# A macaron block's mixer re-ordered: attention A in pairs of row halves beside B's projections, B's attention beside half of the output projection

## The chip, the cores and the metric

The kernel runs on one core of a Trainium2 chip. A core has TensorE (PE in the profile; PEld is its weight load), VectorE (DVE), ScalarE (ACT), GpSimd (POOL) and SyncE (SP, which issues the DMAs). The metric is the device time of one execution in microseconds (us); the time of a kernel is the median of its runs.

## What is computed

One Conformer block on x of 512 rows and 1024 columns, in float32:

```python
x = x + 0.5 * swiglu(rmsnorm(x, ffn1_norm), ffn1_w_gate, ffn1_w_up, ffn1_w_down)
proj = rmsnorm(x, mix_norm) @ w_in          # qa | ka | va | c_q | c_kv | k_rope
qa, ka = rmsnorm per head of 64 (8 heads);  va as it is
out_a = chunked_relbias_attention(qa, ka, va, a_rel_bias)
# B: q = rmsnorm(c_q) @ w_uq (8 heads of 64 + 32), kv = rmsnorm(c_kv) @ w_ukv (8 heads of 64 + 64);
# each part of q and k normed per head, the 32 columns rotated (rope)
out_b = mla_attention(c_q, c_kv, k_rope, ..., w_uq, ..., w_ukv, ...)
x = x + concatenate([out_a, out_b]) @ w_out
x = x + 0.5 * swiglu(rmsnorm(x, ffn2_norm), ffn2_w_gate, ffn2_w_up, ffn2_w_down)
x = rmsnorm(x, final_norm)
```

Both attentions are causal in chunks of 64 rows. A adds a learned bias to the scores, B only the mask.

## The kernel before

Every float32 operand of a product is split into a high part (rounded to the matmul's own type) and a low part (the rest), and `mm3` (L146) makes a product of three matmuls: high by high, high by low, low by high. A weight comes in by `wunit` (L136): one DMA into a `raw` tile (four of them), a copy on ACT for the high part, a subtraction on POOL, or on DVE where `lo_on` says so, for the low part. `whi` and `wlo` have four buffers each.

The kernel has three stages: FFN1 (L207 to L244), the mixer (L248 to L578) with the output projection (L589 to L599), and FFN2. The change is in the middle stage, which lies between 367.6 us and 622.8 us of the profiled span. Its order before:

- `in_proj` (L314) makes four PSUM banks (one for each 128 rows) of one slice of `w_in`. The slices come in this order: the latents (L334), A's queries (`qk_proj`, L377), A's keys (L433), A's values (`values_proj`, L442). PSUM has 8 banks; `bank` (L309) gives a projection four of the banks that the attention will use, in two groups.
- Between A's queries and A's keys stand B's projections: `latents_T` (L358) transposes the normed latents into `latT`; L384 to L404 make B's queries in 8 steps (six matmuls, a copy on ACT, a square on POOL, L396, two sums on DVE, L397 and L398), then the norms (`factors`, L276) and on POOL the scaling (L403) and `rope` (L291, seven POOL instructions, L294 to L304); L407 to L431 make B's keys and values in 8 steps, with a square (L420) and the scaling of the keys (L431) on POOL. The low parts of these weights are made on DVE.
- `factors` calls `rsqrt` (L112): a Ln and an Exp on ACT, each with a table load, and four small DVE instructions.
- The loop at L569 runs over 16 heads, A's eight and then B's eight. For a head, `front` (L468) transposes queries and keys and splits them (`evac`, L460), and for A loads the bias by a DMA and turns its sign on DVE (L482); `softmax` (L507) makes four blocks of scores and for each the bias and the minimum on DVE (L522), the exponential on ACT (L524), the reciprocal on DVE (L525) and the scaling on POOL (L526); `flip` (L529) transposes the probabilities (L542) and splits them on ACT and DVE (L547, L548); `values` (L552) multiplies with the values. In one turn the loop issues the flip of a head, the softmax of the next, the front of the one after, and the values of the one before.
- A's score matmuls use 64 rows of the array: heads with an even number the lower half of the partitions, heads with an odd number the upper half.
- The output projection (L589) has eight steps of 24 matmuls. After each come the residual sum (L595), the split of the new x for FFN2 (L596, L597) and its square (L599, `add_square`).

The framework orders each engine's instructions when the kernel is built, from a priority by the program's order (`high_priority(offset=150)` puts some ahead) and a model of when operands are there. On the chip each engine runs its own list in that order.

Of the kernel before, what the change touches and what calls it, by code (L numbers as in the profile page):

```python
# [11 lines left out]
F32R = mybir.dt.float32r  # L12
AF = mybir.ActivationFunctionType
# [4 lines left out]
P = 128  # L18
# [12 lines left out]
BIG = 1e30  # L31

# [7 lines left out]
def tile_macaron_block(  # L40
# [206 lines left out]
    AH, AL = XH, XL  # L247
    with tc.tile_pool(name="mix", bufs=1, side="left", reuse_waits="tile") as mp:  # L248
        latT = mp.tile([P, 6, S], F32R, tag="vAh", name="latT")
        VBh = mp.tile([P, NT, 4, 192], F32R, tag="vBh", name="VBh")  # L250
        qA = mp.tile([P, NT, 512], F32, tag="qA", name="qA")
        VBl = mp.tile([P, NT, 4, 192], F32R, tag="vBl", name="VBl")
        kA = mp.tile([P, NT, 512], F32, tag="kA", name="kA")
# [3 lines left out]
        for t in (VBh, VBl):  # L257
            pool.memset(t[:, :, :, HD:2 * HD].bitcast(F32), 0.0)
# [6 lines left out]
        rtmp = mp.tile([P, 2560], F32, tag="vAl", name="rtmp")  # L265
        qt = rtmp[:, 0:2048].rearrange("p (t h w) -> p t h w", t=NT, h=NH)
        rtab = rtmp[:, 2048:2560].rearrange("p (i t n w) -> p i t n w", i=2, t=NT, n=4)
# [5 lines left out]
        dve.tensor_scalar(out=nq[:, 0:1], in0=g(C_AQ), scalar1=-(HD ** -0.5), scalar2=None, op0=ALU.mult)  # L273
        dve.tensor_scalar(out=nq[:, 1:2], in0=g(C_BQ), scalar1=-(QK ** -0.5), scalar2=None, op0=ALU.mult)

        def factors(ss, n, width, scaled, name):  # L276

            f = mp.tile([P, NT, n], F32, tag="f_" + name, name="f_" + name)
            y = mp.tile([P, NT, n], F32, tag="y_" + name, name="y_" + name)
            y2 = mp.tile([P, NT, n], F32, tag="z_" + name, name="z_" + name)  # L280
            if scaled:
                dve.tensor_tensor(out=f, in0=ss, in1=vtok.unsqueeze(2).broadcast_to([P, NT, n]), op=ALU.mult)
                dve.tensor_scalar(out=f, in0=f, scalar1=1.0 / width, scalar2=EPS, op0=ALU.mult, op1=ALU.add)
            else:
                dve.tensor_scalar(out=f, in0=ss, scalar1=1.0 / width, scalar2=EPS, op0=ALU.mult, op1=ALU.add)
            rsqrt(f, f, y, y2)
            if scaled:
                dve.tensor_tensor(out=f, in0=f, in1=rtok.unsqueeze(2).broadcast_to([P, NT, n]), op=ALU.mult)
            return f
# [16 lines left out]
        with tc.tile_pool(name="ps2", bufs=1, space=PSUM, reuse_waits="tile") as ps:  # L306
            NB = {"s": 2, "tr": 2, "t": 3, "pv": 1}

            def bank(group, i, name):  # L309

                tag = (("s",) * NB["s"] + ("tr",) * NB["tr"], ("t",) * NB["t"] + ("pv",) * NB["pv"])[group][i]
                return ps.tile([P, 512], F32, tag=tag, name=name, bufs=NB[tag])

# [20 lines left out]
            pts = in_proj(0, LAT, 1)  # L334
            mt = bank(0, 3, "mt")
# [3 lines left out]
            yt = mp.tile([P, NT], F32, tag="yt", name="yt")  # L339
            zt = mp.tile([P, NT], F32, tag="zt", name="zt")  # L340
            rsqrt(rtok, vtok, yt, zt)
# [5 lines left out]
            fcq = factors(ssl[:, 0], 1, 256, True, "cq")  # L347
            fkv = factors(ssl[:, 1], 1, 128, True, "ckv")
            fkr = factors(ssl[:, 2], 1, 32, True, "kr")
# [5 lines left out]
            kt = mp.tile([P, NT, 1, 64], F32, tag="kt", name="kt")  # L355
            rope(kpe[:, :, HD:QK].unsqueeze(2), lat[:, :, 384:416].unsqueeze(2), fkr, 1, 1, kt)

            def latents_T():  # L358
                for j in range(3):
                    pt = bank(1, j, "lt")  # L360
                    for t in range(NT):
                        pe.transpose(pt[:, t * P:(t + 1) * P], lat[:, t, j * P:(j + 1) * P], ident)
                    act.activation(latT[:, 2 * j, :], pt, AF.Copy, scale=g(C_QLAT + j))
                    dve.scalar_tensor_tensor(out=latT[:, 2 * j + 1, :], in0=pt, scalar=g(C_QLAT + j),
                                             in1=latT[:, 2 * j, :].bitcast(F32), op0=ALU.mult, op1=ALU.subtract)

            def qk_proj(off, dst, name):
                pts = in_proj(off, 512, 0)
# [3 lines left out]
                f = factors(ss, NH, HD, True, name)  # L372
# [3 lines left out]

            qk_proj(416, qA, "qa")  # L377
            latents_T()


            qB = mp.tile([P, NT, NH, QK], F32, tag="qB", name="qB")
            ssn = mp.tile([P, NT, NH], F32, tag="ssn", name="ssn")
            ssp = mp.tile([P, NT, NH], F32, tag="ssp", name="ssp")
            for half in range(2):  # L384
                hi, lo = wunit(w_uq[half], 768, dve)
                for t in range(NT):
                    tt = slice(t * P, (t + 1) * P)
                    pt = bank(1, t, "uq")
                    for k in range(2):
                        c = slice(k * 384, (k + 1) * 384)  # L390
                        mm3(pt[:, :384], latT[:, 2 * k, tt], latT[:, 2 * k + 1, tt], hi[:, c], lo[:, c], k == 0, k == 1)
# [44 lines left out]
            def values_proj():  # L436
# [3 lines left out]
                for t in (VAh, VAl):  # L440
                    pool.memset(t[:, :, :, HD:2 * HD].bitcast(F32), 0.0)
# [299 lines left out]
```

## Time and profile before

| what | us |
|---|---|
| median of 3 runs (995.2 to 997.3) | 995.52 |
| the profiled execution | 997.57 |
| its span, first to last instruction | 995.8 |
| of the span, middle stage (367.6 to 622.8) | 255.2 |

| engine, whole span | busy us | share |
|---|---|---|
| PE | 975.5 | 98% |
| DVE | 390.5 | 39% |
| ACT | 391.9 | 39% |
| POOL | 579.6 | 58% |

A busy PE is not PE at its peak: matmuls are pipelined, and the profile's duration of one holds the way through the array. What a matmul costs in a row of them is the distance from one start to the next. The engines' shares are means over stages with different limits, so the middle stage is read by windows.

### The profile page before, as it was taken

The page shows a single profiled execution, that of the slowest core. Times are in us where ns is not written, and L with a number is a line of the kernel's source. Part 1 is how long each engine was busy: PE and PEld are TensorE (multiplying, and loading weights), DVE is VectorE, ACT ScalarE, POOL GpSimd, SP SyncE. Part 2 cuts the span into 40 slices and gives each one's busy share as a digit, 9 for nine tenths or more (in the row PEclk, how much of TensorE's full clock was granted, in tenths as well). Part 3 has the DMA queues.
Part 4 walks back from the last instruction along what each step waited for, and adds up shares of the span by engine and source line. Part 5 has one row for each costly group of instructions (what it writes and reads, how often), then busy time and mean ns, then how long its engine had stood idle before and what let it go on. Part 6 is the DMA issues. An engine that isn't in the chain of part 4 may idle for free.

```text
span 995.8 us, 12076 instructions
## 1 busy us (share of the span) xinstructions
PE 975.5 (98%) x4579; PEld 812.1 (82%) x4579; DVE 390.5 (39%) x684; ACT 391.9 (39%) x661; POOL 579.6 (58%) x424
## 2 busy tenths in 40 slices
PE   9999999999999999898999999999999999999996
PEld 6888888888888889786778978888888888888886
DVE  7533333333121233866788845143333333200002
ACT  7533323232222236563778853343233232322321
POOL 4776666765555530385445567587666667645541
PEclk9999999999999999999999999999999999999998
DMA  6432223233233242220110062323322232333302
GB/s 233 145 109 86 102 89 106 85 106 95 83 102 93 89 141 75 85 64 1 32 33 2 1 212 88 103 86 106 102 88 99 93 104 80 101 96 95 101 16 85
DMA packets 29146, 89.90 MB, mean 90 GB/s; under 512 B 3488, under 2 KB 5664, under 8 KB 29088
## 3 DMA queue, kind: packets, MB, share of 16 engines
q1 hardware_dynamic: 28224, 88.34, 27.6%
q8 instruction: 36, 0.59, 0.2%
q10 hardware_dynamic: 864, 0.79, 0.2%
q14 instruction: 22, 0.18, 0.1%
HBM read 87.02 MB, written 2.10 MB: 89 GB/s over the span
## 4 chain that ended last, share of the span: by engine, by line
PE 89%; DVE 4%; ACT 3%; POOL 2%; issue 1%; DMA 1%; SPq 0%; POOLq 0%; ACTq 0%; DVEq 0%
PE gu L147 15%; PE gu L149 15%; PE gu L148 15%; PE dn L147 8%; PE dn L149 8%; PE dn L148 8%; PE pj L149 2%; PE pj L147 2%; PE pj L148 2%; PE wo L147 1%; PE wo L149 1%; PE wo L148 1%; PE t L542 1%; PE s L147 1%; PE tr L457 1%
## 5 line engine op out<-in xcount | busy, mean ns | idle before, releaser
L143 POOL TENSOR_TENSOR wlo<-raw,whi 128x1024 fp32r<-128x1024 f32 x138 | 324.2, 2350 | 153.3 <-ACT whi L142 152.5
L142 ACT CAST whi<-raw 128x1024 fp32r<-128x1024 f32 (+2 forms) x159 | 162.4, 1022 | 447.7 <-PE gu L148 244.8
L147 PE MATMUL gu<-x2h,whi 128*128 128x512 f32 x352 | 136.9, 389 | 0.0
L148 PE MATMUL gu<-x2l,whi 128*128 128x512 f32 x352 | 136.8, 389 | 0.0
L149 PE MATMUL gu<-x2h,wlo 128*128 128x512 f32 x352 | 136.8, 389 | 0.0
L148 PE MATMUL gu<-xl,whi 128*128 128x512 f32 x320 | 124.5, 389 | 0.0
L147 PE MATMUL gu<-xh,whi 128*128 128x512 f32 x320 | 124.5, 389 | 0.0
L149 PE MATMUL gu<-xh,wlo 128*128 128x512 f32 x320 | 124.5, 389 | 0.0
L162 POOL TENSOR_TENSOR us<-us,gs 128x512 f32<-128x512 f32 x44 | 57.6, 1310 | 108.7 <-DVE us L160 107.2
L161 DVE SCALAR_TENSOR_TENSOR gs<-th,gs 128x512 f32<-128x512 f32 x44 | 91.1, 2074 | 31.8 <-ACT th L159 31.8
L158 DVE TENSOR_TENSOR gs<-gu,rs 128x512 f32<-128x512 f32 x44 | 30.4, 691 | 175.9 <-PE gu L149 168.7
L191 DVE SCALAR_TENSOR_TENSOR x<-dn,x 128x512 f32<-128x512 f32 (+1 forms) x17 | 11.2, 660 | 193.9 <-PE dn L149 193.9
L148 PEld LDWEIGHTS gu<-x2l,whi 128*128 128x128 f32 x352 | 66.1, 188 | 13.8
L149 PEld LDWEIGHTS gu<-x2h,wlo 128*128 128x128 f32 x352 | 66.1, 188 | 13.8
L147 PEld LDWEIGHTS gu<-x2h,whi 128*128 128x128 f32 x352 | 66.1, 188 | 13.6
L149 PEld LDWEIGHTS gu<-xh,wlo 128*128 128x128 f32 x320 | 60.1, 188 | 12.6
L147 PEld LDWEIGHTS gu<-xh,whi 128*128 128x128 f32 x320 | 60.1, 188 | 12.5
L148 PEld LDWEIGHTS gu<-xl,whi 128*128 128x128 f32 x320 | 60.1, 188 | 12.3
L147 PE MATMUL dn<-h1h,whi 128*128 128x512 f32 x176 | 68.5, 389 | 0.0
L148 PE MATMUL dn<-h1l,whi 128*128 128x512 f32 x176 | 68.5, 389 | 0.0
L149 PE MATMUL dn<-h1h,wlo 128*128 128x512 f32 x176 | 68.5, 389 | 0.0
L160 DVE SCALAR_TENSOR_TENSOR us<-gu,rs 128x512 f32<-128x512 f32 x44 | 30.4, 690 | 64.9 <-PE gu L149 64.9
(327 smaller groups left out, 1864.5 us busy)
## 6 DMA issues: line engine op xcount, KB each, us to landing
raw<-in_gu SPq DMA_DIRECT2D x84, 512.0 KB, 3.6
raw<-in_dn SPq DMA_DIRECT2D x32, 512.0 KB, 3.5
raw<-in_dn SPq DMA_DIRECT2D x16, 384.0 KB, 3.1
raw<-in_w_in SPq DMA_DIRECT2D x12, 512.0 KB, 3.4
raw<-in_w_out SPq DMA_DIRECT2D x8, 512.0 KB, 4.3
x<-in_xT SPq DMA_DIRECT2D x8, 256.0 KB, 5.4
raw<-in_gu SPq DMA_DIRECT2D x8, 256.0 KB, 5.4
bias<-in_bias_tab SPq DMA_DIRECT2D x8, 256.0 KB, 2.7
```

Source lines behind the costliest of these rows:

```text
L142: act.copy(hi[:, :n], raw[:, :n])
L143: (lo_on or pool).tensor_tensor(out=lo[:, :n], in0=raw[:, :n], in1=hi[:, :n].bitcast(F32), op=ALU.subtract)
L147: pe.matmul(out, lhsT=ah, rhs=bh, start=start, stop=False)
L148: pe.matmul(out, lhsT=ah, rhs=bl, start=False, stop=False)
L149: pe.matmul(out, lhsT=al, rhs=bh, start=False, stop=stop)
L158: dve.tensor_tensor(out=gs, in0=gup[0], in1=rs, op=ALU.mult)
L160: dve.scalar_tensor_tensor(out=us, in0=gup[1], scalar=0.5, in1=rs, op0=ALU.mult, op1=ALU.mult)
L161: dve.scalar_tensor_tensor(out=gs, in0=th, scalar=1.0, in1=gs, op0=ALU.add, op1=ALU.mult)
L162: pool.tensor_tensor(out=us, in0=us, in1=gs, op=ALU.mult)
L191: dve.scalar_tensor_tensor(out=x[dt][:, h], in0=pt[:, h], scalar=0.5, in1=x[dt][:, h], op0=ALU.mult, op1=ALU.add)
L457: pe.transpose(pt[0:src(t).shape[1], t * P:(t + 1) * P], src(t), ident)
L542: pe.transpose(tt[:, o + i * P:o + (i + 1) * P], pi[i][:, j * P:(j + 1) * P], ident)
```

## The change

The attention runs over 12 items instead of 16 heads: four pairs of A's heads, then B's eight heads. B's projections leave their place between A's queries and keys; they are cut into steps, and the loop issues the steps in the turns of A's first two pairs. The output projection is cut in two halves: the half that takes A's output is issued in the turns of B's attention, the other half comes where the whole was. The score matmuls of a pair's two heads are issued alternately. `rsqrt` in the mixer becomes a start value from the bits and three Newton steps on DVE (ten instructions). The bias keeps its sign (the DVE instruction turns the sum instead), the reciprocals of a head's four blocks become one, the low parts of B's weights move from DVE to POOL, and rope of B's queries is done in four parts. PSUM's banks are shared out anew.

```diff
+        def rsqrt_small(out, v, w):
+            y, t = (mp.tile([P, 2 * NT * NH], F32, tag="rsq", name="rsq", bufs=2)[:, 0:w] for _ in range(2))
+            dve.tensor_scalar(out=y.bitcast(I32), in0=v.bitcast(I32), scalar1=-0.5, scalar2=RSQ, op0=ALU.mult, op1=ALU.add)
+            for i in range(3):
+                dve.scalar_tensor_tensor(out=t, in0=y, scalar=-0.5, in1=y, op0=ALU.mult, op1=ALU.mult)
+                dve.tensor_tensor(out=t, in0=t, in1=v, op=ALU.mult)
+                dve.scalar_tensor_tensor(out=out if i == 2 else y, in0=t, scalar=1.5, in1=y, op0=ALU.add, op1=ALU.mult)
...
-            NB = {"s": 2, "tr": 2, "t": 3, "pv": 1}
+            NB = {"s": 2, "tr": 1, "t": 2, "pv": 1, "pj": 2}
...
-                tag = (("s",) * NB["s"] + ("tr",) * NB["tr"], ("t",) * NB["t"] + ("pv",) * NB["pv"])[group][i]
+                tag = (("s", "s", "tr", "pv"), ("t", "t", "pj", "pj"))[group][i]
...
+            def queries_b(half, t):
+                if t == 0:
+                    B["w"] = wunit(w_uq[half], 768)
...
+            def norm_q():
...
+                for i in range(4):
+                    hs = slice(2 * i, 2 * i + 2)
+                    rope(qB[:, :, hs, HD:QK], qB[:, :, hs, HD:QK], fp[:, :, hs], 0, NH // 4, qt)
...
+            def out_a(dt):
+                hi, lo = B["o", dt // 2]
+                pt = pj("woa")
+                for c in range(4):
+                    cc = slice((dt % 2) * 512 + c * P, (dt % 2) * 512 + (c + 1) * P)
+                    mm3(pt, hi[:, cc], lo[:, cc], OUT[c][0], OUT[c][1], c == 0, c == 3)
+                dve.tensor_tensor(out=x[dt], in0=pt, in1=x[dt], op=ALU.add)
...
+                    for j, (a, b) in enumerate(((0, 2), (0, 3), (1, 2))):
+                        for o, hd in zip(so, heads):
+                            pe.matmul(o, lhsT=hd[a][:, ii], rhs=hd[b][:, 0:nn], start=j == 0, stop=j == 2)
...
+            values_proj()
+            tiles = [tiles_b]
+            beside = {-1: [lambda j=j: latents_T(j) for j in range(3)],
+                      0: tiles + [lambda i=i: queries_b(i // 4, i % 4) for i in range(8)] + [norm_q],
+                      1: [lambda i=i: keys_values_b(i // 2, i % 2) for i in range(8)] + [norm_k]}
+            for i in range(4):
+                beside.setdefault(4 + i // 2, []).append(lambda i=i: weights_o(i))
+            for dt in range(KD):
+                beside.setdefault(5 + dt, []).append(lambda dt=dt: out_a(dt))
+            fronts = [lambda pr=pr: front_a(pr) for pr in range(4)] + [lambda b=b: front_b(b) for b in range(NH)]
+            n = len(fronts)
...
+            for it in range(-2, n + 1):
+                pis = prob.pop(it, [None])
+                more = beside.get(it, [])
+                for e, pi in enumerate(pis):
+                    cur = None
+                    if pi is not None:
+                        cur = head, flip(pi)
+                        head += 1
+                    if e == 0:
+                        with (tc.high_priority(offset=150) if it < 0 else ExitStack()):
+                            if 0 <= it + 1 < n:
+                                prob[it + 1] = softmax(qk.pop(it + 1))
+                            if it + 2 < n:
+                                qk[it + 2] = fronts[it + 2]()
+                    if last:
+                        values(*last)
+                    last = cur
+                    half = (len(more) + 1) // 2 if len(pis) > 1 else len(more)
+                    for f in more[e * half:(e + 1) * half]:
+                        f()
...
-            hi, lo = wunit(w_out[dt], 1024)
+            if dt % 2 == 0:
+                hi, lo = wunit(w_out[1, dt // 2], 1024)
             pt = ps.tile([P, S], F32, tag="mm", name="wo")
-            for c in range(KD):
+            for c in range(4, KD):
```

`keys_values_b` is L408 to L427 in steps as `queries_b` is L384 to L398, with `wunit(w_ukv, 1024)` and no `dve`; `norm_k` is L428 to L431. `weights_o(i)` loads and splits a quarter of A's half of `w_out` into tiles that A's values and keys held.

## Rows read from the trace of the kernel before

**Rows 1.** Windows: stretch, its length, busy us (count) of PE, PEld, DVE, ACT, POOL, clock, DMA share, GB/s

```profile
408.60:482.00 73.40, 66.25 (x309) 54.62 (x308) 49.15 (x113) 40.22 (x83) 39.54 (x37) 0.98 0.10 32
482.00:526.00 44.00, 42.87 (x264) 32.76 (x263) 37.91 (x133) 33.67 (x99) 23.21 (x49) 1.00 0.14 37
526.00:579.20 53.20, 52.38 (x353) 46.87 (x352) 43.92 (x154) 44.20 (x123) 28.34 (x54) 1.00 0.12 40
579.20:622.80 43.60, 43.60 (x195) 36.14 (x194) 22.61 (x15) 17.09 (x25) 34.24 (x18) 1.00 0.40 126
```

**Rows 2.** Waits of PE, 367.5 to 623: us in total, times, longest

```profile
PE tr L457 <- DVE kA L375: 4.2, 1, 4.2
PE pj L147 <- DVE qA L375: 1.2, 1, 1.2
PE uq L147 <- ACT latT L363: 0.9, 1, 0.9
PE uq L147 <- DVE latT L364: 0.8, 1, 0.8
```

**Rows 3.** Timeline of PE in A's attention: start us, us, engine, line, operation, count

```profile
488.71 0.44 PE L147 MATMUL s<-xh,xh 64*128 64x384 f32 x1
489.00 0.33 PE L148 MATMUL s<-xl,xh 64*128 64x384 f32 x1
489.17 0.34 PE L149 MATMUL s<-xh,xl 64*128 64x384 f32 x1
489.44 0.33 PE L542 MATMUL t<-ident,pa 128*128 128x128 f32 x1
...
493.11 0.49 PE L147 MATMUL s<-xh,xh 64*128 64x512 f32 x2
493.34 0.49 PE L148 MATMUL s<-xl,xh 64*128 64x256 f32 x2
```

**Rows 4.** Groups on POOL, 367 to 580: count, busy us, mean ns, idle before

```profile
L526 POOL TENSOR_TENSOR pa<-pa,sm 128x512 f32<-128x512 f32 (+1 forms) x32 | 29.7, 932 | 38.2 <-DVE sm L525 37.6
L526 POOL TENSOR_TENSOR pb<-pb,sm 128x256 f32<-128x256 f32 (+1 forms) x32 | 16.2, 505 | 13.5 <-DVE sm L525 13.5
L396 POOL TENSOR_TENSOR sqq<-qB 128x384 f32<-128x384 f32 x8 | 7.5, 950 | 12.7 <-DVE z_qa L117 9.2 <-DVE ssp L398 3.5
L420 POOL TENSOR_TENSOR sqk<-kB 128x256 f32<-128x256 f32 x8 | 5.8, 742 | 3.8 <-DVE z_qp L116 3.8
L403 POOL TENSOR_TENSOR qB<-qB,f_qn 128x512 f32<-128x512 f32 x4 | 5.0, 1286 | 0.2 <-DVE f_qp L119 0.2
L143 POOL TENSOR_TENSOR wlo<-raw,whi 128x1024 fp32r<-128x1024 f32 x2 | 4.7, 2386 | 3.2 <-ACT whi L142 3.2
L299 POOL TENSOR_TENSOR rtmp<-rtmp 128x512 f32<-128x512 f32 x1 | 2.3, 2270 | 0.0
L303 POOL TENSOR_TENSOR rtmp<-rtmp 128x512 f32<-128x512 f32 x1 | 1.3, 1289 | 0.0
```

**Rows 5.** Groups on DVE, 367 to 580, same columns

```profile
L525 DVE RECIPROCAL sm<-sm 128x1 f32<-128x1 f32 x64 | 9.0, 151 | 1.3 <-ACT pb L524 0.6 <-ACT pa L524 0.5
L482 DVE TENSOR_SCALAR bias<-bias 128x512 f32<-128x512 f32 x8 | 4.7, 585 | 1.3 <-DMA bias<-in_bias_tab 1.2
L427 DVE TENSOR_TENSOR VBl<-ukv,VBh 128x128 fp32r<-128x128 f32 x16 | 4.0, 279 | 0.1
L117 DVE TENSOR_TENSOR z_kn<-z_kn,f_kn 128x32 f32<-128x32 f32 x1 | 1.2, 1216 | 0.0
L117 DVE TENSOR_TENSOR z_ka<-z_ka,f_ka 128x32 f32<-128x32 f32 x1 | 0.2, 193 | 0.0
```

**Rows 6.** Groups of the whole span on DVE, in the output projection

```profile
L597 DVE SCALAR_TENSOR_TENSOR x2l<-x,col,x2h 128x512 fp32r<-128x512 f32 x8 | 19.4, 2431 | 6.5 <-ACT x2h L596 6.5
L595 DVE TENSOR_TENSOR x<-wo,x 128x512 f32<-128x512 f32 x8 | 5.5, 692 | 14.6 <-PE wo L149 14.6
```

**Rows 7.** DMA issues, page part 6: KB each, us to landing

```profile
raw<-in_w_in SPq DMA_DIRECT2D x12, 512.0 KB, 3.4
```

More of the change, by code (lines that the diff above doesn't have):

```diff
@@ L272, in tile_macaron_block @@
         nq = mp.tile([P, 2], F32, tag="nq", name="nq")
[L273 to L280, printed above, removed]
-            if scaled:
[L282 to L289, printed above, removed]
+        dve.tensor_scalar(out=nq[:, 0:1], in0=g(C_AQ), scalar1=HD ** -0.5, scalar2=None, op0=ALU.mult)
@@ new lines, in factors @@
+        def factors(parts, n, scaled, name):
+            w = len(parts) * NT * n
+            f = mp.tile([P, len(parts), NT, n], F32, tag="f_" + name, name="f_" + name)
+            for i, (ss, width) in enumerate(parts):
+                src = ss
+                if scaled:
+                    dve.tensor_tensor(out=f[:, i], in0=ss, in1=vtok.unsqueeze(2).broadcast_to([P, NT, n]), op=ALU.mult)
+                    src = f[:, i]
+                dve.tensor_scalar(out=f[:, i], in0=src, scalar1=1.0 / width, scalar2=EPS, op0=ALU.mult, op1=ALU.add)
+            flat = f.rearrange("p i t n -> p (i t n)")
+            rsqrt_small(flat, flat, w)
+            if scaled:
+                for i in range(len(parts)):
+                    dve.tensor_tensor(out=f[:, i], in0=f[:, i], in1=rtok.unsqueeze(2).broadcast_to([P, NT, n]), op=ALU.mult)
+            return [f[:, i] for i in range(len(parts))]
@@ L354, in tile_macaron_block, with qk_proj @@
                 act.copy(lat[:, t, 384:416], pts[t][:, 384:416])
[L355 to L368, printed above, removed]
+            rope(kpe[:, :, HD:QK].unsqueeze(2), lat[:, :, 384:416].unsqueeze(2), fkr, 1, 1, qt[:, :, 0:1, :])
+            def qk_proj(off, dst, name, group):
+                pts = in_proj(off, 512, group)
                 ss = mp.tile([P, NT, NH], F32, tag="ss_" + name, name="ss_" + name)
@@ L375, in qk_proj @@
                     dve.tensor_tensor(out=dv, in0=pts[t].rearrange("p (h w) -> p h w", w=HD), in1=f[:, t, :].unsqueeze(2).broadcast_to([P, NH, HD]), op=ALU.mult)
[L377 to L391, printed above, removed]
-                    hs = slice(4 * half, 4 * half + 4)
-                    pv = pt[:, :384].rearrange("p (h w) -> p h w", w=QK)
-                    act.copy(qB[:, t, hs, :], pv)
-                    sq = work.tile([P, 512], F32, tag="wb", name="sqq")[:, :384].rearrange("p (h w) -> p h w", w=QK)
-                    pool.tensor_tensor(out=sq, in0=qB[:, t, hs, :], in1=qB[:, t, hs, :], op=ALU.mult)
-                    dve.tensor_reduce(out=ssn[:, t, hs], in_=sq[:, :, 0:HD], op=ALU.add, axis=AX.X)
-                    dve.tensor_reduce(out=ssp[:, t, hs], in_=sq[:, :, HD:QK], op=ALU.add, axis=AX.X)
@@ L428, in tile_macaron_block @@
[L428 to L433 removed]
+            qk_proj(416, qA, "qa", 1)
+            qk_proj(416 + 512, kA, "ka", 0)
             def values_proj():
[L438 to L441 removed]
```

275 lines of the change are left out of this document (152 added, 123 removed).

## The prediction

> **What bounds the kernel now.** I read the windows first, then the waits of PE, then the timeline, and last the groups on POOL and DVE. The windows [rows 1] cut the middle stage after the second projection: 73.4 us with B's projections and the rest of A's, 44.0 us of A's attention, 53.2 us of B's, 43.6 us of output projection. PE is busy in 42.9 of 44.0 us, in 52.4 of 53.2 and in all of 43.6, so three of the four stretches are already bound by PE. Only the first has a hole: 66.3 of 73.4 us. The waits [rows 2] name it: 4.2 us for A's keys, 1.2 for A's queries, 0.9 and 0.8 for the latents, 7.1 us in all. DVE comes second in both attentions (37.9 of 44.0, 43.9 of 53.2), ACT is close behind, and POOL is only half used (23.2 of 44.0). In the projections POOL works 39.5 us, beside PE, without PE waiting for it.
>
> So there are two things to win: the hole, and PE's own work. Putting work beside B's attention wins almost nothing by itself, because PE has no hole there to fill.
>
> **Waits of PE, gain 5.1.** Without B's steps between them, A's projections follow each other; while one is finished on ACT and DVE the next runs, in the other group of banks. The latents and A's queries are then waited for by nobody: 0.9 + 0.8 + 1.2 us go. A's keys still end in a chain before the first transposes, and these are put ahead of A's values by priority. The chain loses two table loads on ACT and gains six small DVE instructions of 0.19 us [rows 5]; I leave 2 of the 4.2 us standing, with 0 and 4.2 as bounds. Sum 7.1 - 2 = 5.1.
>
> **Clock, gain 1.5.** The granted clock is 0.98 over the first 73.4 us [rows 1], a part of it at the lower level, 1.2 GHz, after PE had stood for 4.2 us [rows 2]. At full clock the same work is shorter by 0.02 x 73.4 = 1.5 us. With 2 us of wait I take it as gone; it costs 0 to 1.5 if it is not.
>
> **Pairs of row halves, gain 5.5.** A matmul of 512 columns costs 43.6 / 192 = 0.227 us in a row of them [rows 1], one of 384 columns 0.17 [rows 3], one of 256 about 0.114, half of 512. A head's scores are 3 x (0.227 + 0.17 + 0.114 + 0.114) = 1.9 us, eight heads 15.0. The timeline [rows 3] shows two matmuls on different row halves under one count at 493.11, and the next starts 0.23 us later, the time of the longer one alone: they run together. The change makes all of them pairs of equal size, 15.0 / 2 = 7.5 us less. Ten such pairs arise by chance before and hide some 2 us already, so 5.5.
>
> **Change of row mode, gain 4.** The block at 488.71 [rows 3] has starts 0.29, 0.17 and 0.27 us apart, where 0.17 each would do: 0.22 us for going in and out, and the entry ahead of it is not in these rows. I take 0.25. There are 32 such blocks before and 16 after: 16 x 0.25 = 4 us.
>
> Together PE's path gets shorter by 5.1 + 1.5 + 5.5 + 4 = 16.1 us.
>
> **B's projections beside A's attention, cost 18.** PE's own work only moves: 48 matmuls of 384 columns, 24 of 512 and 12 transposes, 15 us. What lay beside it moves too, and there it had cover: in the 73.4 us stretch PE never waited for POOL. Now the same POOL work stands in the list beside the scaling of A's probabilities, and the next flips wait for that. POOL's list from the end of A's values to the last of A's probabilities [rows 4]:
>
> - scaling of three pairs: (29.7 + 16.2) / 16 = 2.87 us a head, six heads 17.2;
> - squares for queries and keys 7.5 + 5.8 = 13.3;
> - scaling of B's queries 5.0, and of the keys, four instructions of the same size, 5.0, together 10.0;
> - rope, seven instructions: 9.0 at 1.29 us each, 15.9 at 2.27; in quarters each pays its start four times. The two scaling groups (932 ns for 448 columns on the mean, 505 for 192) give 0.18 us of start, 21 x 0.18 = 3.8 more. I take the lower end, 13, since the slow ones stood beside DVE's low parts of weights, which are not made in this stretch any more;
> - low parts of three weights, new on POOL: 2.4 and, at three quarters of it, 2 x 1.8, together 6.
>
> That is 59.5 us. It can't begin at once: the first weight of B's needs a raw tile that the first flip gives back, then its DMA (3.4 us [rows 7]) and the copy on ACT; with the flip and the queue ahead I take 8 us. The steps also hang on each other: queries, sums, `factors`, scaling, rope, and only then B's first front; I add 2 us for the two chains of small DVE instructions. So the stretch lasts 59.5 + 8 + 2 = 69.5 us. PE has in it: A's 44.0, less 9.5 for pairs and modes, less about 1.5 of waits already in it, plus 15 for B's projections, plus some 4 of B's first fronts and scores, 52. The difference is a stall of 17.5, say 18. Bounds: 6 if POOL's work slips into gaps and DVE is next, 28 if rope takes its higher price and the chains run slowly. DVE in the same stretch: 37.9, less sign and reciprocals (about 7 heads x (0.585 + 3 x 0.151) = 7), plus B's 16 splits of 0.28 (4.5) and, as an estimate from these rows, 15 for 24 sums, three larger splits and 24 small instructions, plus 4 for the splits of A's values [rows 5]: 54, below POOL but close.
>
> While POOL sets this stretch the pairs win nothing in it: a shorter PE only waits longer. That is why the stall is as large as it is.
>
> **A's half of the output projection beside B's attention, gain 1.** 96 matmuls x 0.227 = 21.8 us move from one stretch that PE fills to another that PE fills. They can take the 0.8 us that PE stands there [rows 1] and the wait at its end. Bounds 0 and 2.5. The eight residual sums are issued twice, 8 x 0.69 us [rows 6] more on DVE, beside PE.
>
> **What is left of the output projection, cost 1.5.** It takes 21.8 us of PE, but each of its eight steps still has the residual sum and the split on DVE, 0.69 + 2.43 us [rows 6], 25 us in all, against 2.7 us of PE a step. Before, DVE had 5.4. FFN2's first products need the last split only some 5 us after the last step, so 25 + 2.7 - 21.8 - 5 is about 1; POOL's sums of squares and weight splits are as dense (34.2 of 43.6 us before, of which not even half goes). I take 1.5, bounds 0 and 5.
>
> **Sum.** -16.1 + 18 - 1 + 1.5 = +2.4 on the profiled execution of 997.57 us (995.8 of span and 1.8 around it), 1000.0. The profiled execution is 2.05 us above the median of the runs, 995.52; the predicted median is 998.0 us, slower by 0.25%. About 0.2%, 2 us, is what a measurement of this kernel can tell from no change.
>
> **A rule that speaks against the change.** An instruction of 32 columns on DVE took 0.19 us while POOL stood and 1.22 us while POOL worked [rows 5]. The Trainium skill, page "SBUF — State Buffer", section "Who interferes with whom", says that a DVE instruction with two SBUF inputs and a GpSimd instruction that reads SBUF exclude each other, and the later one waits for the whole of the earlier. The trace agrees in these two rows.
>
> **Rivals.**
>
> 1. *The lists interleave* (faster). The framework puts an instruction into any gap of POOL in which it is ready, so A's scaling may slip between the steps of rope, and A's attention runs on while B's norms trail; DVE at 54 us then sets the stretch against PE's 52, and the stall is 4 to 8 us instead of 18. For it: POOL has only 23.2 of 44 us now, and DVE ran at 86% beside a PE that hardly waited [rows 1]. Against it: B's fronts can't start before all of POOL's work on B is done, and until A ends no step of the output projection can fill in. It decides for faster when the stall is under 13 us. Time: 998.0 - 12 = 986, up to 992.
> 2. *DVE's Newton steps stand behind POOL* (slower still). 24 instructions of the two norms sit on the way to B's first front; at 0.6 us on the mean instead of 0.19 (halfway to 1.22) they add 10 us: 1008. With one bank for transposes instead of two and two for flips instead of three, similar small waits could add up to the same.
> 3. *The pairs do not run together*, because two heads need both score banks at each block and one waits for the other's evacuation. PE then keeps 5.5 to 9.5 us, but inside a stretch that POOL sets, so the time stays within 997 to 1003; it would only be seen in the timeline.
>
> **How the numbers follow.** Chances: the forecast with rival 3, 0.50 (994 to 1003); rival 1, 0.33 (985 to 993); rival 2, 0.17 (1004 to 1012). The range 986 to 1009 leaves out a tenth on either side. Faster by over 0.2% (below 993.5): 0.34, rival 1 nearly whole. Within it (to 997.5): 0.20. Slower: 0.46.
>
> **What would show it.** In the changed profile: no wait for latents or A's queries, at most one of about 2 us for A's keys; score matmuls in twos at the same start, 0.23 us for a 512 pair; from the end of A's values to the first flip of B some 70 us with POOL at 85% or more and PE waiting for POOL's scaled probabilities or for what follows B's norms, 15 to 20 us in all; PE over 97% busy in B's attention, now some 72 us long; a short wait at FFN2's start. The forecast is wrong if POOL is below 75% there, or if PE's waits in it are under 10 us.

## The result and the profile after

The changed kernel takes 1009.45 us at the median (1008.72 to 1014.49) against 996.35 for the kernel before (four runs, three of them those of the table above), a ratio of 1.0143 with a 95% interval of 1.0107 to 1.0179. Run once more, unaltered, it took 1014.44 (1009.93 to 1017.53), ratio 1.0179 (1.0157 to 1.0200). It is slower, as forecast, but by 13 to 18 us where I had forecast 2.4; both medians lie above the range, 986 to 1009, the first by half a microsecond and the second by 5. The profiled execution of the first took 1008.72 us with a span of 1006.9 (1.8 around it).

The windows after, cut where the projections, A's attention, B's attention and the rest of the output projection end; columns as in [rows 1]:

```profile
366.50:451.50 85.00, 85.00 (x400) 73.47 (x400) 43.66 (x114) 25.09 (x44) 8.79 (x21) 1.00 0.20 64
451.50:535.20 83.70, 70.52 (x402) 55.22 (x401) 62.52 (x191) 54.10 (x155) 56.92 (x97) 0.92 0.14 45
535.20:612.60 77.40, 71.94 (x420) 61.77 (x419) 46.04 (x130) 46.80 (x120) 44.38 (x66) 0.98 0.14 48
612.60:634.30 21.70, 21.70 (x98) 17.98 (x97) 14.72 (x13) 11.92 (x18) 18.07 (x12) 1.00 0.38 123
```

The projections, with the waits of [rows 2] in them before, now run without a gap, and so does the rest of the output projection. All the loss lies between: PE stands (it has nothing to run) 83.7 - 70.5 = 13.2 us in A's attention and 5.5 in B's, and the granted clock is 0.92 and 0.98 there. The waits of PE in A's attention:

```profile
PE tp L592 <- DVE PAl L595: 4.4, 2, 3.3
PE ukv L149 <- DVE VBl L460: 3.2, 1, 3.2
PE tp L592 <- POOL pa L574: 2.0, 3, 1.1
PE s L566 <- DVE mn L568: 1.0, 2, 0.7
```

The longest, 3.3 us before a flip, in the timelines of POOL, DVE and PE (start, us, ...):

```profile
503.92 0.68 DVE L568 CUSTOM_DVE_ANT_0 pa<-s,bias 128x512 f32<-128x512 f32 x1
...
515.72 0.17 DVE L572 RECIPROCAL sm<-sm 128x4 f32<-128x4 f32 x1
516.30 0.17 DVE L572 RECIPROCAL sm<-sm 128x4 f32<-128x4 f32 x1
...
517.35 1.82 POOL L574 TENSOR_TENSOR pa<-pa,sm 128x512 f32<-128x512 f32 x2
519.13 0.61 POOL L574 TENSOR_TENSOR ssum<-ssum,sm 128x256 f32<-128x256 f32 x1
...
520.71 1.82 POOL L574 TENSOR_TENSOR pa<-pa,sm 128x512 f32<-128x512 f32 x2
522.49 0.61 POOL L574 TENSOR_TENSOR ssum<-ssum,sm 128x256 f32<-128x256 f32 x1
523.06 0.39 POOL L574 TENSOR_TENSOR pa<-pa,sm 128x128 f32<-128x128 f32 x1
...
521.92 3.67 DVE L298 TENSOR_SCALAR f_kn<-ssk 128x32 f32<-128x32 f32 x1
526.40 0.68 DVE L595 TENSOR_TENSOR PAl<-tp,PAh 128x512 fp32r<-128x512 f32 x1
...
518.44 0.55 PE L592 MATMUL tp<-ident,pa 128*128 128x128 f32 x3 [1.15 <-POOL pa L574]
521.28 0.69 PE L592 MATMUL tp<-ident,pa 128*128 128x128 f32 x2 [1.16 <-DVE PAl L595]
527.14 0.69 PE L592 MATMUL tp<-ident,pa 128*128 128x128 f32 x2 [3.28 <-DVE PAl L595]
```

Read it from the top. The largest block of the pair is taken from its scores at 503.92, but both heads' reciprocals come at 515.72 and 516.30, after the last exponential of all four blocks; so that block is scaled 13.4 us after its scores were read, and eight scalings of two heads stand on POOL in one lump from 517.35 on. PE's flips wait for them. In the kernel before, a block of this size is scaled 2.5 us after its scores were read:

```profile
488.97 0.68 DVE L522 CUSTOM_DVE_ANT_0 pa<-s,bias 128x512 f32<-128x512 f32 x1
...
491.46 1.04 POOL L526 TENSOR_TENSOR pa<-pa,sm 128x512 f32<-128x512 f32 x1 [0.17 <-DVE sm L525]
```

While POOL works through lump and rope without a gap (520.1 to 525.6), one DVE instruction of 32 columns takes 3.67 us and ends with POOL's row, at 525.59 (0.17 for its like at 496.3); and the split that gives the flip bank back stands behind it: 3.28 us for PE.

Then the clock, in the three stretches that lie at 1.2 GHz:

```profile
503.10:506.50 3.40, 3.40 (x13) 2.69 (x11) 3.25 (x11) 2.03 (x6) 3.40 (x5) 0.50 0.01 2
520.10:530.40 10.30, 5.85 (x21) 4.67 (x21) 8.28 (x19) 2.46 (x6) 7.18 (x14) 0.50 0.16 52
608.90:612.30 3.40, 3.39 (x10) 2.69 (x11) 0.55 (x1) 0.58 (x1) 2.94 (x2) 0.50 0.70 255
```

The first comes right behind PE's 3.2 us before the keys' matmuls, the second lies around the 5.6 us of waits just shown, and the third comes behind two waits of 1.2 and 1.4 us at the end of B's attention.

**The balance of the middle stage** (first projection to the last matmul of the output projection; 255.2 us before, 267.8 after). PE's matmuls at full clock, counted at what each costs in a row of its like, are the same 232 us in both, an estimate from the timelines. The cuts before are 481.2, 538.8 and 579.3; the two attentions and the one stretch at 1.2 GHz before are

```profile
481.20:538.80 57.60, 56.34 (x349) 44.54 (x349) 49.45 (x174) 44.71 (x130) 29.29 (x61) 1.00 0.10 29
538.80:579.30 40.50, 39.81 (x272) 35.88 (x271) 33.17 (x116) 34.03 (x95) 22.36 (x42) 1.00 0.15 53
465.00:468.40 3.40, 2.70 (x11) 2.54 (x12) 1.91 (x4) 1.37 (x2) 0.00 (x0) 0.50 0.00 0
```

The loss at 1.2 GHz is half of what PE worked in those stretches; "rest" is what remains beyond work, waits and clock: changes of row mode and small gaps, less what pairs hide.

| us | predicted change | before | after | change |
|---|---|---|---|---|
| PE stands in the projections | -5.1 | 7.2 | 0 | -7.2 |
| lost at 1.2 GHz | -1.5 | 1.4 | 6.3 | +4.9 (run 7's execution +10.0) |
| rest (pairs, row mode) | -9.5 | 12.6 | 10.8 | -1.8 |
| PE stands in A's attention | +18 | 1.3 | 13.2 | +11.9 |
| PE stands in B's attention | -1 | 0.7 | 5.5 | +4.8 |
| rest of the output projection | +1.5 | 0 | 0 | 0 |
| sum | +2.4 | | | +12.6 |

(The whole span grew by 11.1 us; the stages on either side are together 1.5 us shorter in this execution.)

### The profile page after: what moved, and what is told of

It reads as the page before. It is cut to its first block, busy times and chain, and to the rows that moved or that the text cites. A ratio compares the mean times of both kernels' runs of the same rounds, so it can differ in the third digit from the quotient of the medians.

```text
span 1006.9 us, 12017 instructions
## 1 busy us (share of the span) xinstructions
PE 976.9 (97%) x4579; PEld 812.4 (81%) x4579; DVE 385.3 (38%) x657; ACT 372.7 (37%) x629; POOL 577.0 (57%) x448
## 5 line engine op out<-in xcount | busy, mean ns | idle before, releaser
L145 POOL TENSOR_TENSOR wlo<-raw,whi 128x1024 fp32r<-128x1024 f32 (+1 forms) x137 | 320.8, 2342 | 145.5 <-ACT whi L144 144.1
L144 ACT CAST whi<-raw 128x1024 fp32r<-128x1024 f32 (+2 forms) x155 | 158.0, 1020 | 441.2 <-PE gu L150 242.1
L151 PEld LDWEIGHTS gu<-x2h,wlo 128*128 128x128 f32 x352 | 66.1, 188 | 13.7
L149 PEld LDWEIGHTS gu<-xh,whi 128*128 128x128 f32 x320 | 60.1, 188 | 12.6
L574 POOL TENSOR_TENSOR pa<-pa,sm 128x512 f32<-128x512 f32 (+2 forms) x48 | 35.5, 754 | 44.4 <-DVE sm L572 44.3
```

The lines of the kernel that those rows point to most:

```text
L144: act.copy(hi[:, :n], raw[:, :n])
L145: (lo_on or pool).tensor_tensor(out=lo[:, :n], in0=raw[:, :n], in1=hi[:, :n].bitcast(F32), op=ALU.subtract)
L149: pe.matmul(out, lhsT=ah, rhs=bh, start=start, stop=False)
L151: pe.matmul(out, lhsT=al, rhs=bh, start=False, stop=stop)
L574: pool.tensor_tensor(out=pi[i], in0=pi[i], in1=sm[:, i:i + 1].broadcast_to([P, (i + 1) * P]), op=ALU.mult)
```

## Experiments

Theories, as named in the expectations: **lock** (POOL shuts out DVE's small instructions, DVE's queue stands, PE with it, and the clock falls), **amount** (POOL has too much to do), **banks** (two score banks keep pairs apart and few flip banks make waits), and later **lists** (the lump of reciprocals and scalings).

**1. B's factors on POOL** (`norms_pool`).

```diff
-dve.tensor_scalar(out=f[:, i], ...); rsqrt_small(flat, flat, w)
+pool.tensor_scalar(out=f[:, i], ...); pool.tensor_tensor(out=flat, in0=flat, in1=-0.5, op=pow)
```

> The factors of B's norms (24 small instructions on DVE) are worked out on POOL instead, by three tensor_scalar and two power instructions; all else is as in the changed kernel. Theory 'lock': the two long stalls of PE in A's attention (3.2 us before the keys' matmuls, 3.3 us before a flip) come from DVE's small instructions, which POOL shuts out and behind which DVE's queue stands; they go, and with them the stretch at 1.2 GHz that follows the second (10.2 us, so 5 us lost) and the one that follows the first (3.4 us, 1.7 lost). 1009.4 - 6.5 - 5 to 7 = 996 to 999. Theory 'amount': POOL's list is what A's attention waits for, and it gets five instructions more: 1009 to 1012.

Measured 1019.96 us, ratio 1.0232 (1.0216 to 1.0247). It tests neither theory: the power instruction itself is slow, 10.55 us for 64 columns and 5.44 for 32, and now PE waits for B's keys:

```profile
502.84 10.55 POOL L306 TENSOR_TENSOR f_qb<-f_qb,mhf 128x64 f32<-128x64 f32 x1
```

```profile
PE tr L500 <- POOL kB L472: 6.1, 4, 5.0
```

The two long waits did shrink, the flips' from 3.3 to 1.2 and the keys' from 3.2 to 1.0.

**2. B's factors on ACT** (`norms_act`): `Ln` and `Exp` for the 24 small instructions; the correcting step is left out.

> The factors of B's norms come from three Ln and two Exp instructions on ACT (without the correcting step that the kernel before has after them) instead of 24 small instructions on DVE; POOL's list is that of the changed kernel. Theory 'lock': the long stalls before the keys' matmuls (3.2 us) and before a flip (3.3 us) go, with about 5 us of the clock's loss behind them; table loads on ACT (1.28 us each) give back 2 to 3: 1000 to 1004. Theory 'amount': POOL's list is unchanged, so the time is too: 1007 to 1011.

1005.31 us, 1.0089 (1.0065 to 1.0114), 4 to 9 us less than the changed kernel's two medians and between the two ranges. Of A's standing only 2 us went (13.2 to 11.1), so the rest of the difference may be the clock's (see run 7):

```profile
PE ukv L149 <- DVE VBl L469: 1.7, 1, 1.7
PE tp L601 <- DVE PAl L604: 1.5, 2, 1.2
```

**3. B's scalings on DVE** (`scale_dve`): `pool` becomes `dve` in the scalings of `norm_q` and `norm_k`.

> The eight multiplications that scale B's queries and keys by their norms (4.1 and 4.0 us on POOL) are done on DVE, everything else as in the changed kernel. Theory 'amount': the sixteen microseconds that a slow power instruction put on POOL cost 10.5 us, so eight taken off give 4 to 6 back: 1003 to 1006. Theory 'lock': DVE's queue gets eight instructions of two SBUF inputs that POOL shuts out, and is longer than before: 1008 to 1013.

1014.48 us, 1.0170 (1.0139 to 1.0201). Eight us off POOL give nothing: PE stands 13.5 us as before. By itself this does not refute "amount", since DVE got the work; run 15, with the same work on POOL and 8 us less standing, does. The DVE instruction that took 3.67 us takes 0.17 here, and PE stands no less; so that one stall is not what the standing hangs on.

**4. B's projections moved back** (`bproj_back`): `latents_T`, `queries_b`, `norm_q`, `keys_values_b` and `norm_k` are called ahead of A's keys, with the weights' low parts on DVE.

> B's projections (latents, queries, keys and values, their norms, with the low parts of their weights on DVE) stand between A's queries and A's keys again, as in the kernel before; pairs, Newton's steps and A's half of the output projection stay as changed. Theories 'lock' and 'amount': the loss lies in this move. PE's waits in A's attention go (13 of 18.6 us) with 5 us of clock, and the waits before the projections come back (7 us): 1009.4 - 18 + 7 = 998, 996 to 1001. Theory 'banks': the loss lies in the two score banks, the two flip banks and the end of B's attention, which all stay: 1005 to 1009.

998.74 us, 1.0026 (1.0016 to 1.0036): 1.0143 - 1.0026, 11.7 us in a thousand, hang on this move. But PE still stands 5.3 and 4.3 us in the two attentions, 1.3 and 0.7 before.

**5. The output projection whole** (`out_whole`), as in the kernel before, and **6. no alternation of heads** (`unpaired`: the loops over heads and over the three products change places).

> The output projection is whole again, behind both attentions; nothing of it lies beside B's attention. My prediction gave this part of the change 1 us of gain and 1.5 us of cost; the trace after shows the second half of the output projection without waits, so by 'lock' and 'amount' undoing it costs 0 to 2 us: 1009 to 1012. If A's half instead delays B's attention (its weights' low parts on POOL, its residual sums on DVE), undoing it gains 2 us or more: below 1007.

> Each head's three score products of a block run in a row, with no matmul of the other row half between them. In the trace after, 23 of 48 possible pairs ran together and hide 3.4 us of PE. If PE sets A's attention, this costs 3 us: 1012 to 1013. If POOL or DVE sets it ('lock', 'amount'), PE only waits less: 1008.5 to 1010. If the alternate order holds the first head's evacuation back ('banks'), it gains 1 to 2 us: 1007 to 1008.

1016.21 us, 1.0184 (1.0156 to 1.0212), and 1012.65, 1.0166 (1.0149 to 1.0183). PE stands in A's attention 13.4 and 13.7 us, what it stands in the changed kernel; only the clock differs, 0.83 and 0.86 where that had 0.92, and 0.87 in run 7. So neither difference can be put down to the edit. Without the alternation 28 pairs still start together, against 23: the planner mixes the heads by itself.

**7. The changed kernel again** (`after_again`).

> The changed kernel once more, unaltered, for its time and its clock: its instruction lists are the same in every execution, so a difference is the chip's. If the clock's part is a matter of chance, its runs spread over 1008 to 1015 and the stretches at 1.2 GHz lie elsewhere in this profile; if it follows from the order, they lie at the same places (about 503, 520 and 609 us) and the time stays at 1009.

```profile
451.60:540.10 88.50, 74.91 (x402) 58.47 (x401) 62.67 (x191) 54.32 (x155) 57.54 (x99) 0.87 0.14 42
...
502.10:515.70 13.60, 12.84 (x41) 9.76 (x42) 7.02 (x25) 6.65 (x21) 7.05 (x12) 0.50 0.00 1
526.00:536.20 10.20, 6.46 (x26) 5.33 (x25) 7.08 (x16) 1.70 (x4) 7.08 (x13) 0.50 0.17 53
```

The same standing (13.6 us), but at the same wait near 502 the clock falls for 13.6 us instead of 3.4. With a third stretch of 3.4 us this execution loses 11.4 us at 1.2 GHz where the first lost 6.3. The clock falls at nearly the same points of the order, but not for the same time; that makes up 5 of the 5.7 us between the two profiled executions, and a difference of this size is no evidence for an edit in runs 2, 3, 5, 6 and 8. The Trainium skill, page "TensorE: Matmul & The Clock Gate", section "Part 1: The HAM clock gate", says that the monitor's phase is not tied to the kernel, so that one kernel differs from run to run. The two profiles agree in that they differ; that the phase is the reason, no run here shows.

**8. Keys' and values' matmuls twice** (`keys_values_twice`: the `mm3` in `keys_values_b` is issued a second time into the same bank).

> The changed kernel with the 24 matmuls of B's keys and values issued twice (each second one overwrites the first, same numbers): 5.4 us more work for PE in the stretch where it stands. If PE sets that stretch: 1014 to 1015. If POOL and DVE set it, the extra work only fills waits: the waits fall by 3 to 5 us, the time stays within 1007 to 1011. If the lower clock follows from PE's standing, the time at 1.2 GHz (16.9 us of the span's middle stage) falls too, and the run may be 1 to 3 us faster in spite of more work: 1006 to 1009.

1011.64 us, 1.0149 (1.0132 to 1.0166), between the changed kernel's own medians, so the time alone can't tell. The standing can: it falls from 13.2 to 6.9 us in A's attention and grows from 5.5 to 7.4 in B's, 4.3 us less in all for 5.4 us of extra work. So most of the work goes into waits, and PE alone doesn't set these stretches. The low clock did not shrink (0.92 again). The planner lays the lists anew around the added work, so the single waits can't be compared one by one.

**9. Both moves undone** (`moves_undone`), and from there **10. four score banks** (`moves_undone_4s`: `s` 4, `tr` 1, `t` 2, `pv` 1) and **11. the banks of before** (`pairs_old_banks`: `s` 2, `tr` 2, `t` 3, `pv` 1).

> The order of the kernel before (B's projections ahead of A's keys, the output projection whole at the end), with the pairs of row halves, Newton's steps and the changed banks kept. By the sizes of my prediction pairs and changes of row mode give 9.5 us here, where POOL does not set the stretch: 987 to 989. By what the trace after shows (3.4 us hidden by 23 pairs against 2.05 by 10, 19 blocks of 64 rows against 25 at 0.2 us each) they give 2.5, less some small waits for the fewer transpose and flip banks: 993 to 998.

> As the run with both moves undone, but with four banks for scores and no bank of their own for projections, so that the second head's block has a free bank when the first head's starts. Theory 'banks': two score banks keep the pairs apart; now 40 or more of 48 run together, the hidden time goes from 3.4 to about 7 us, and the run is 3 to 5 us faster than the one with two banks. If DVE's evacuations or the order on PE keep them apart: within 1 us of it.

> As the run with both moves undone, but with the kernel before's banks too (two for scores, two for transposes, three for flips, one for values): of the change only the pairs, Newton's steps and quartered rope are left. If the fewer transpose and flip banks ate the pairs' gain (waits 12.0 us there against 9.1 before), it is 2 to 3 us below that run, 994 to 995. If the pairs are worth nothing even so: 996 to 997.5. My prediction's sizes would give 987.

996.97 us, 1.0005 (0.9996 to 1.0014): pairs, Newton's steps, the new banks and the one reciprocal for four blocks, all of which stay in this run, are together worth nothing (run 16 tells the reciprocal apart). With four score banks (run 10) 35 of 48 pairs start together instead of 20, among them ten of the twelve of 384 columns, of which run 9 has none; the rest of the balance falls from 11.8 us to 7.7. So free score banks do let more pairs run, which fits the Trainium skill (page "TensorEngine Tiling (Array Packing)", section "Gotcha 1: PSUM Pressure": row tiles need different PSUM banks). But the banks are not the whole reason: run 11, with two of them, pairs six of the twelve,

```profile
487.67 0.45 PE L584 MATMUL s<-xh,xh 64*128 64x384 f32 x2
487.95 0.34 PE L584 MATMUL s<-xl,xh 64*128 64x384 f32 x2
488.12 0.34 PE L584 MATMUL s<-xh,xl 64*128 64x384 f32 x2
```

and 19 of 48 in all, so the order that the planner gives the matmuls has a part in it too. And run 10 takes 1009.59, 1.0131 (1.0115 to 1.0148): PE stands 19.8 us in its middle stage against run 9's 12.1 and loses 10.3 us at 1.2 GHz against 1.7. The largest of the new waits are at the bank for transposes, now the only one:

```profile
PE tr L500 <- DVE ql L505: 3.4, 3, 1.1
PE tr L500 <- DVE qk L505: 1.6, 1, 1.6
PE tr L500 <- DVE xl L505: 1.0, 1, 1.0
```

The old banks (run 11) give 1000.24, 1.0036 (1.0023 to 1.0049): more flip and transpose banks do not help, and "banks" does not explain the standing in the attentions (4.5 and 4.0 us in run 9, 3.9 and 5.0 here; 1.3 and 0.7 before).

**12. A's keys early** (`keys_early`: in the kernel before, `qk_proj` of the keys follows that of the queries), **13. the same with pairs** (`keys_early_pairs`), **14. first transposes later** (`first_later`: `high_priority(offset=40)` for 150 in the kernel before).

> The kernel before with one thing moved: A's keys are projected straight after A's queries, and B's projections follow, ahead of A's values. No work goes beside the attention. My prediction's first step, alone: the waits for A's keys, A's queries and the latents (7.1 us) go, since another projection lies behind each, and 1.4 us of clock with them: 988 to 991. If B's norms beside A's values and first scores stall PE as they do beside A's attention: 995 to 1000.

> The two runs above together: pairs with the kernel before's banks, and A's keys ahead of B's projections. If both gains stand and add: 985 to 989. If only the keys' place gains: as that run, within 2 us.

> The kernel before with one number changed: the first fronts and scores get a lower priority, so that the transposes of A's queries and keys stand some 19 matmuls of A's values later in PE's list, past the point at which A's keys are there. The wait of 4.2 us and the 1.4 us of clock behind it go: 991 to 993. If the first scores then come too late for DVE and POOL and the attention starts with a wait of its own (as when A's keys were projected early): 996 to 999.

997.86, 1.0016 (1.0007 to 1.0026); 1003.23, 1.0071 (1.0047 to 1.0094); 996.88, 1.0007 (0.9997 to 1.0017). The wait of 4.2 us [rows 2] is gone from all three, and none is faster. It comes back a step later: as 3.8 us before a second pair's transposes (481.2) in run 12, and in run 14 as

```profile
PE pv L147 <- ACT PAh L547: 1.7, 1, 1.7
PE t L542 <- DVE PAl L548: 1.5, 1, 1.5
```

(The profiled executions of runs 12 and 14, at 1001 us, have 13.7 us at 1.2 GHz each, where the kernel before has 3.4.) In these three runs a wait ahead of a chain was not won by taking it away; that the chain from A's keys to the first scaled probabilities is what keeps its length is the likely reading, and was not measured by itself.

**15. Reciprocals per block** (`recip_each`) and **16. the same without the moves** (`moves_undone_recip`).

```diff
                         act.activation(pi[i], pi[i], AF.Exp, ...)
-                for pi, mn, sm in out:
-                    dve.reciprocal(sm, sm)
-                    for i in (3, 2, 1, 0):
-                        pool.tensor_tensor(out=pi[i], in0=pi[i], in1=sm[:, i:i + 1]..., op=ALU.mult)
+                        dve.reciprocal(sm[:, i:i + 1], sm[:, i:i + 1])
+                        pool.tensor_tensor(out=pi[i], in0=pi[i], in1=sm[:, i:i + 1]..., op=ALU.mult)
```

> The changed kernel, but each block's probabilities get their reciprocal and their scaling straight after their own exponentials, as in the kernel before, and not all four blocks after the last. Theory 'lists' (PE waits because the scaling of a head comes late and in one lump on POOL, and the flips after it): the waits in A's attention (13.1 us) and at the end of B's (5.4) fall by 4 to 8 us in all: 1002 to 1006. Theory 'lock': DVE gets 3 x 12 more small instructions that POOL can shut out: 1009 to 1013.

> The same edit in the kernel with both moves undone, whose attentions wait 4.4 + 3.9 us where the kernel before waits 1.2 + 0.7. If the lump of reciprocals and scaling makes these waits, they fall to under 3 us and the time to 991 to 994. If it is the two flip banks and the changed order of flips: 996 to 998.

1001.53 us, 1.0050 (1.0038 to 1.0062), and 994.66, 0.9980 (0.9970 to 0.9989). Run 15 lies just under the range of "lists", run 16 just above its own. With B's move (below) this is the largest piece of the loss, 8 to 13 us (the larger against the changed kernel on the same chip, 1014.44). Windows of run 15, then its timeline of DVE and POOL:

```profile
451.70:523.60 71.90, 67.16 (x389) 53.25 (x388) 59.70 (x212) 52.57 (x152) 52.63 (x91) 0.98 0.16 52
523.60:605.10 81.50, 74.62 (x432) 62.93 (x431) 51.03 (x157) 48.63 (x122) 49.50 (x72) 0.97 0.13 43
```

```profile
498.95 0.68 DVE L568 CUSTOM_DVE_ANT_0 pa<-s,bias 128x512 f32<-128x512 f32 x1
...
501.86 1.04 POOL L572 TENSOR_TENSOR pa<-pa,sm 128x512 f32<-128x512 f32 x1 [1.25 <-DVE sm L571]
504.41 1.04 POOL L572 TENSOR_TENSOR pa<-pa,sm 128x512 f32<-128x512 f32 x1 [1.51 <-DVE sm L571]
506.03 1.61 POOL L572 TENSOR_TENSOR pa<-pa,sm 128x384 f32<-128x384 f32 x2 [0.58 <-DVE sm L571]
507.59 1.19 POOL L572 TENSOR_TENSOR ssum<-ssum,sm 128x256 f32<-128x256 f32 x2
...
519.47 0.24 DVE L298 TENSOR_SCALAR f_kn<-ssk 128x32 f32<-128x32 f32 x1
```

The scalings now come block by block, the largest 2.9 us after its scores were read instead of 13.4; the DVE instruction that took 3.67 us takes 0.24; PE stands 4.7 us in A's attention instead of 13.2. DVE has 48 more reciprocals and is none the worse, and POOL is busy as long as before in the two attentions together (102.1 us, 101.3 in the changed kernel). "Lists" holds; "lock" was one of the ways in which the lump reached PE. The edit moves two things, the merged reciprocals and the place of the four scalings in the program; the run does not tell them apart.

**17. and 18. The other two corners** (`recip_out_whole`, `recip_bproj_back`).

> With the reciprocals per block: B's projections beside A's attention (as changed), the output projection whole at the end. With the two runs that have both moves (1.0050 of the kernel before) and neither (0.9980) it makes a table of two by two with the next run. If A's half beside B's attention is worth what the difference of the two runs without B's move showed (998.7 against 997.0, a cost of 1.8): 999 to 1000.5. If it fills PE's waits in B's attention (6.8 us there in the run with both), leaving it out costs 2 to 5: 1003 to 1006.

> With the reciprocals per block: B's projections ahead of A's keys as before, A's half of the output projection beside B's attention (as changed). If that half costs 1.8 us as without this edit: 996 to 997. If it fills the 4.4 us that PE waits in B's attention in the run with neither move: 991 to 993. The rest of the difference to the run with both moves (1001.5) is what B's move costs once the lump is gone: 4.5 or 9 us.

With reciprocals per block, ratio to the kernel before:

| | B's projections as before | beside A's attention |
|---|---|---|
| output projection whole | 0.9980 (0.9970 to 0.9989) | 1.0059 (1.0046 to 1.0073) |
| A's half beside B's attention | **0.9938** (0.9926 to 0.9951) | 1.0050 (1.0038 to 1.0062) |

B's move costs 8 to 11 us even without the lump. A's half beside B's attention gains 4 us with B's projections as before, and beside B's move 1, which the intervals do not tell from nothing; with the lump and B's projections as before it costs 2 (runs 4 and 9, 1.0026 and 1.0005). Read as a path from the changed kernel to the kernel before, in us: the lump 9 to 13, A's half -1, B's move 8, and -2 for what is left (pairs, Newton's steps, banks), 14 to 18 in all. The bold corner, 990.0 us (989.43 to 991.2), beats both kernels. Its windows:

```profile
365.80:469.50 103.70, 100.83 (x484) 87.50 (x483) 70.82 (x183) 38.45 (x82) 47.85 (x74) 1.00 0.20 65
469.50:531.00 61.50, 58.90 (x373) 46.16 (x373) 50.43 (x181) 48.72 (x140) 32.02 (x65) 1.00 0.13 40
531.00:593.40 62.40, 60.42 (x363) 52.79 (x362) 39.61 (x121) 38.80 (x96) 32.19 (x42) 1.00 0.16 53
```

The clock stays at 1.00 throughout, and PE stands 2.9 + 2.6 + 2.0 us.

## Why the prediction was right or wrong

**Slower, for another reason and by more.** The stall beside A's attention came (12 us, forecast 18), but not as forecast, and that its size is near is luck. I had POOL's list set the stretch, at 85% or more; POOL was busy 56.9 of 83.7 us, 68%, which I had named as the sign that the forecast is wrong. DVE, which I put at 54 us and below POOL, was busy 62.5. With the same work on POOL, run 15 took 8.5 us of the stall away.

**The step that failed: what sets A's attention, and in it the reciprocals.** The change gathers each head's four reciprocals in one instruction behind the last exponential. I booked that as seven microseconds off DVE, together with the sign, and put the wait it adds at nothing: every scaling of a head now waits for its last block, and the scalings of both heads of a pair come in one lump. By run 15 that is 8 to 13 us; undone without the moves it is 2.3 (run 16 against 9). In the terms of the sum, A's stall and the waits in the projections came out 8.2 us better than forecast and the rest of the output projection 1.5; pairs and row mode missed by 7.7, the clock by 6.4 (11.5 in run 7's execution) and B's attention by 5.8. These three follow. For them the time went up although the stall, at 12 us, met the condition that rival 1 set for a faster kernel (under 13).

**Pairs and row mode, 9.5 forecast, 1.8 found.** The sizes of one pair and one change were near: 256-column products of two heads start together and the next follows 0.12 us on,

```profile
506.69 0.44 PE L566 MATMUL s<-xh,xh 64*128 64x384 f32 x1
...
507.41 0.50 PE L149 MATMUL pv<-PAh,VAh 128*128 128x512 f32 x1
507.84 0.44 PE L566 MATMUL s<-xh,xh 64*128 64x384 f32 x1
...
510.95 0.29 PE L566 MATMUL s<-xl,xh 64*128 64x256 f32 x2
511.07 0.29 PE L566 MATMUL s<-xh,xl 64*128 64x256 f32 x2
```

but only 23 of 48 pairs form. Of the 384-column products none do: in the first rows other work lies between the two heads'. Runs 10 and 11 show the score banks as one reason and the order as another. The 23 pairs hide 3.3 us; the ten of the kernel before, a 512 with a 256 each, hid 1.1 (ten times 0.114), not 2. The stretches of 64-row products fall from 25 to 19, not from 32 to 16. Rival 3 named this and put it inside the forecast because POOL would set the stretch. In the balance the missing gain counts, but by run 8 much of it would only have made PE wait longer here. In run 16, without either move or the lump, the pairs and all that is left of the change win 2 us.

**The clock, -1.5 forecast, +5 to +10 found.** I took the low clock as gone with the 4.2 us wait and gave the new stall none. The stretches at 1.2 GHz lie behind or around the longer waits, and of five executions with 13.2 to 13.7 us of standing in A's attention the granted clock there was 0.92, 0.87, 0.83, 0.86 and 0.86.

**B's attention, -1 forecast, +4.8 found.** PE was to be over 97% busy there; it was 93% (71.9 of 77.4 us). Of the 5.5 us 3.7 stand in the last 11 us, before flips and values of the last heads, the longest 1.4 us before values for ACT's last split. A wait of 1.46 us at that place is in runs 9, 15, 16 and 18 as well, so with and without either move and the lump; no wait of PE in B's attention before is longer than 0.3 us. Which of the edits that these runs share brings it was not tried, and run 11 has it with the old banks (2.9 us).

**Rival 2, DVE's small instructions behind POOL**, gave 1008 and is the nearest in the number. Its mechanism is in the trace (3.67 us for one instruction, 0.32 to 0.96 for Newton's steps at 497 to 501), and run 2, which takes these steps off DVE, is 4 to 9 us faster with 2 us less standing; but it takes the lump to make it matter. The rule I set beside it explains part: the Trainium skill, page "SBUF — State Buffer", section "Who interferes with whom", counts `tensor_scalar` among the instructions that can want the shared ports, and lets the later one wait for the whole of the earlier. Here the instruction took as long as some ten POOL instructions in a row, the longest of them 0.9 us, more than the whole of one.

**Waits of PE in the projections**: 7.1 us forecast to shrink to 2, and they went to 0. Yet runs 12 to 14, which take 4 to 5 of these 7 us away, win nothing, since the time is lost again in the attention. That step was right in the trace, and no run shows it worth anything in the time.

**Rest of the output projection**: 1.5 forecast, no wait found; the half runs in 21.7 us, all PE. **A's half beside B's attention**: 1 forecast; with reciprocals per block 4 without B's move and 1 with it, and -2 with the lump and without B's move.

**What stays open**: of the 8 to 11 us that B's move still costs with reciprocals per block, the windows of the four corners show 2 to 4 us more standing in A's attention, 3 to 5 more in B's, 3 less in the projections, and some 5 us more lost at the lower clock; which of B's instructions make these waits was not tried further, nor what makes those of B's attention that come without either move.

## What to carry to other kernels

Ask of an instruction that replaces four small ones what its latest input is, and who waited for the earliest of its outputs: here it cost more than anything it saved. A stall of PE can cost the clock besides itself: 6 to 11 us here beside 19 us of standing, and at most 2 beside the 10 to 12 of runs 9 and 16. And a move of work beside other work is worth testing by halves: with the lump gone, one of the two here gained 4 us by itself and the other lost 8 or more.

## What was not expected of the hardware

A power instruction on POOL takes about 0.165 us a column (10.55 us for 64, 5.44 for 32), where a multiplication of 256 columns takes 0.61. A DVE instruction of 32 columns, 0.17 us elsewhere, took 3.67 us beside some ten POOL instructions in a row and ended with the last of them. And of the same instruction list, at the same wait, PE's clock stayed at 1.2 GHz for 3.4 us in one execution and for 13.6 in another.
